# The low parts of streamed weights: a DMA that adds onto rounded weights, in place of a subtraction on VectorE

## The chip, the cores and the metric

One core of one Trainium2 chip runs the whole program in one launch. The metric is the device time in microseconds of that launch; lower is better. The core has TensorE (PE; its weight loads are listed as PEld), VectorE (DVE), ScalarE (ACT), GpSimd (POOL) and SyncE (SP). SP and POOL are the two engines from which this kernel issues nearly all of its DMAs.

## The reference, cut to what matters

Two transformer-like blocks over 512 tokens of width 1024, all in float32:

```python
# block 1: chunked attention + pooled branch, gated, then a conv-gated feed-forward
h = rms_norm(x, norm_mix_pre)
q, k, v, u, gates = split(h @ w_in)
y_a = chunk_band_attention(q, k, v, rel_bias) @ w_attn_out
y_b = multiscale_pool(u, w_pool_group, pool_scale) @ w_pool_out
g_a, g_b = split(sigmoid(gates + b_gate))
x = x + rms_norm((g_a * y_a + g_b * y_b) @ w_o, norm_mix_post)
f = conv_gated_ffn(rms_norm(x, norm_ffn_pre), w_up, conv_w, conv_b, w_down)
x = x + rms_norm(f, norm_ffn_post)
# block 2: gated delta rule + differential attention side by side
proj = rms_norm_2(x, w_norm) @ w_in_2
o_a = gated_delta_rule_chunked(...)      # needs the inverse of (I + L) of each chunk
o_b = diff_attention(...)
x = x + concat(o_a, o_b) @ w_out_2
```

Every large product is weights (about 20 million float32 numbers in all) against 512 tokens.

## The kernel before, in words

**Products in three parts.** A float32 operand is split in two numbers of the type that TensorE multiplies fast (fp32r): `hi`, the rounded value, and `lo`, the value minus `hi`. A product is then three matmuls on the same PSUM bank, in the order hi·ahi, hi·alo, lo·ahi (`mm3`). So of each 128 rows of a weight piece, the low part is wanted by the third matmul.

**The weight stream.** All weights come in 157 pieces in the order of use (`weight_order`), most of them 128 x 1024 (512 KB), those of the down-projection 128 x 1024 and 128 x 896. A piece goes through three steps:

- `fetch` loads it from HBM into a raw tile on SP's queue; there are two raw tiles, so a load waits until the piece two before it has been split.
- `split_next` makes `whi` from the raw tile with ACT (`split_hi`, a copy that rounds) and `wlo` with DVE (`split_lo`, raw minus `whi`), and then calls `fetch` for the next load. There are four `whi` and four `wlo` tiles.
- `take` hands the pair to the products. `weights` takes a piece and calls `advance`, which starts the split of the piece two further on. The split is thus begun about when the piece two before it starts on TensorE.

Six pieces that follow a seam (`early`) are split in halves into other tiles, and seven of the last product's pieces are split in two unequal parts. The first two pieces of the program are split half by half while they arrive, by code of their own.

**What sets the order.** Each engine works through its instructions in the order in which they were issued. `Issue` keeps estimated times and runs the background tasks (generators) when their operands should have come; a task pauses while ACT or DVE is more than `SLACK` us ahead. The estimates decide only that order. On the chip, each instruction waits for its operands, and what stands behind it on its engine waits too.

**The beginning.** The first two pieces (`w_qk`) are multiplied as they and `x` arrive. The next pieces, four of `w_v`, come through the stream; each product with them is token-major (`gemm_tok`): 256 columns at a time, with k = 0 to 3 from one piece and k = 4 to 7 from the next, so both are wanted at once. Beside it `first_norm` squares `x` on ACT and sums it on DVE and POOL (`acc`), and five loads of `rel` are issued on POOL's queue.

**The seams.** Between the two halves of a block, and between the blocks, the norm needs a whole product. There `Seam.chain` works through the tokens in two halves, and `seam_products` multiplies what is ready. The chain uses DVE (three steps for each of 8 k), ACT and, for the sum of squares, POOL. Two pieces are split under the second half.

**POOL in block 2.** Each of two `gdn_pair` tasks inverts 16 x 16 triangular blocks by substitution: 30 short POOL instructions (`cb`, `xt`) that depend on one another and are issued all together. A DMA (`dx`) then carries the result on, and TensorE needs it. Also on POOL's queue: the eight stores of `x` to DRAM after the second seam, their reload (`xr`) before the last product, and the stores of the output.

Of the kernel before, what the change touches and what calls it, by code (L numbers as in the profile page):

```python
# [13 lines left out]
ALU = mybir.AluOpType  # L14
# [15 lines left out]
# block 2's projections in order: a and z are feature-major tiles, the others two heads token-major  # L30
UNITS = ["a6", "a10", "a4", "a1", "a8", "a7", "a3", "a5", "a2", "a9", "q1", "v0", "a0", "q0",
         "k0", "z5", "a11", "k1", "z3", "z0", "z2", "z4", "z1", "z6", "z7", "v1"]
# heads in the order in which the last product takes them: the first of them in all tiles, then the others
# [7 lines left out]
# issue order: a task goes on when its last results are LEAD us away, unless an engine has SLACK us of work  # L41
# [23 lines left out]
def weight_order():  # L65
    """(array, piece, first column, end) in the order of use"""
    o = []

    def add(name, i=None, a=0, b=None):
        o.append((name, i, a, b))  # L70

    for hp in range(4):
        add("w_qk", 2 * hp)
        add("w_qk", 2 * hp + 1)
        if hp == 0:
            for i in range(4):
                add("w_v", i)
    add("w_pg")
    for i in range(4):
        add("w_u", i)  # L80
    for m in range(KD):
        add("w_g", 2 * m)
        add("w_g", 2 * m + 1)
        add("w_ap", m)
    for m in range(KD):
        add("w_o", m)
    for i in range(2 * MF):
        add("w_up", i)
    for m in range(KD):
        for a, b in ((0, 8), (8, 15), (15, 22)):  # L90
            add("w_dn", m, a * P, b * P)
    for u in UNITS:
        if u[0] in "az":
            add("w2_" + u[0], int(u[1:]))
        else:
            add("w2_" + u, 0)
            add("w2_" + u, 1)
    for m in range(KD):
        add("w_out", m)
    return o  # L100
# [5 lines left out]
class Issue:  # L106
    """Order of issue. Each engine works through its instructions in the order in which they are issued;
    the times that are kept here, in us, are estimates and decide that order alone."""
# [45 lines left out]
    def issue(self, e, op, outs, ins, func=None):  # L154
        self.count += 1
        lat = {"PE": 0.2, "V": 0.13, "A": 0.13, "G": 0.13}[e]
        start = max(self.free[e], self.ready(*ins) + lat)
        if e == "PE":
            start = max(start, self.now)
        # one engine at a time works on a PSUM bank  # L160
        held = [self.bank.setdefault(x.name, {}) for x in (*outs, *ins) if x.space == PSUM]
        for d in held:
            start = max([start] + [t + 0.05 for o, t in d.items() if o != e])
        if func in TABLES and TABLES[func] != self.table:
            self.table = TABLES[func]
            start += 1.28
        t = start + self.cost(e, op, outs, ins)
        for d in held:
            d[e] = t
        self.free[e] = t  # L170
        if e == "PE":
            self.now = t
        self.done(outs, t + (0.05 if e == "PE" else 0.0))
# [16 lines left out]
    def step(self):  # L190
        """tasks whose results have come go on; between two yields a task's work is issued together"""
        for task in list(self.tasks):
            if task[0] > self.now + LEAD:
                continue
            if not task[2] and max(self.free["V"], self.free["A"]) > self.now + SLACK:
                continue
            self.mark = task[3]
            r = next(task[1], "end")
            if r == "end":
                self.tasks.remove(task)  # L200
            else:
                task[0], task[3] = self.now if r == 0 else self.mark, self.mark
# [13 lines left out]
class Engine:  # L216
    """An engine whose instructions are counted by an Issue."""
# [18 lines left out]
def kernel(ctx, tc, aps, out, dbg=None):  # L236
# [13 lines left out]
    # PSUM banks: of each kind the time at which a bank's last readers are done  # L250
# [21 lines left out]
    # ---- background tasks: generators; "yield" waits for what was just issued, "yield 0" does not  # L272
# [3 lines left out]

    def move(dst, src):
        """a transfer within the chip's memories"""
# [3 lines left out]
    def grab_all(tag, n):  # L282
        """PSUM banks whose last readers are done"""
# [70 lines left out]
    # ---- weight stream: fetched three pieces ahead, split two ahead  # L354
# [16 lines left out]
    def split_next():  # L371
        while not raws:
            yield
        key, raw, n = raws.pop(0)
        yield from after(raw)
# [7 lines left out]
        elif key[0] == "w_out" and key[1] < NPART:  # L383
            # the first heads' weights pass through, the others' stay
# [8 lines left out]
        else:  # L393
            hi = wp.tile([P, n], F32R, tag="whi", name="whi", bufs=4)
            lo = wp.tile([P, n], F32R, tag="wlo", name="wlo", bufs=4)
            split_hi(raw, hi)
            yield
            split_lo(raw, hi, lo)
        done.append((key, hi, lo))
        fetch()  # L400

    def take(name, i=None, a=0, b=None):
# [3 lines left out]
        until(lambda: done)  # L406
# [4 lines left out]
    def weights(*key):  # L411
        """the next piece of the stream"""
# [9 lines left out]
    def wcol(w, k):  # L422
        """the weights of one k, of a piece that may wait in two halves"""
        return w[k // 4][:, k % 4 * P:(k % 4 + 1) * P] if isinstance(w, list) else w[:, k * P:(k + 1) * P]

    def mm(ps, w, x, start, stop):
        """a slice of a large product; while its operands are on their way other work goes on"""
# [34 lines left out]
    def copy(dst, src, scale=None):  # L462
        """on the engine that is free first"""
# [7 lines left out]
    def scale_rows(t, r):  # L471
        """t[p, c] *= r[p, c]"""
# [21 lines left out]
    def rstd(acc, col, tbs):  # L494
        """col[token] = 1 / rms and the same spread over the partitions"""
# [10 lines left out]
    class Seam:  # L506
        """x += rms_norm(f) and the next operand x * g split in two parts, one half of the tokens at a
        time: the norm of the first half runs under the products of the second."""
# [61 lines left out]
    def project_norm(wkeys, hi, lo, gname, seam, gnext):  # L570
        """f = W^T act in 8 output tiles; wkeys(m) lists each tile's pieces and their k ranges"""
# [27 lines left out]
    # ------------------------------------------------------------------ block 1: mixer  # L599
    # the first two products begin while their operands arrive  # L600
# [16 lines left out]
    # the tensor engine's clock rises while it works  # L617
# [60 lines left out]
    def attn_item(h, qb):  # L678
        """scores and softmax of (head, 128 queries)"""
# [40 lines left out]
    def attn_values():  # L720
        """transposed probabilities times values, (head pair, 128 keys) at a time"""
# [46 lines left out]
    def stack_q(src):  # L768
        """two heads of 64 features: for each its high part and, in the other half of the partitions, its low part"""
# [9 lines left out]
    def stack_k(src):  # L779
        """for each of two heads its high part in both halves, and their low parts"""  # L780
# [10 lines left out]
    def score(ps, q, k, j, qs, n):  # L791
        """(q_hi + q_lo) k_hi, then q_hi k_lo"""
# [59 lines left out]
    # pooling branch  # L852
# [44 lines left out]
    # gates, branch outputs, their mix  # L897
# [45 lines left out]
    # ------------------------------------------------------------------ block 1: feed-forward  # L943
# [37 lines left out]
    def seam_products(sn, keys, finish):  # L981
        """the first products after a seam, one half of the tokens at a time"""
# [72 lines left out]
    # inverses of the blocks of 16 x 16 go into zeros  # L1055
# [11 lines left out]
    # ------------------------------------------------------------------ block 2  # L1067
# [8 lines left out]
    def delta_gates():  # L1076
        """decays and write strengths, column c * 4 + h"""
# [74 lines left out]
    def gdn_pair(hs):  # L1152
        """two heads of the delta rule; chunks of 128 tokens. k, q and v carry a factor 2 from silu."""
# [12 lines left out]
        def decays():  # L1166
            """the chunks' running log decays on all partitions"""
# [41 lines left out]
        # the diagonal blocks of 64 x 64 of the chunks: [128, NT, 64], rows 0-63 one block, rows 64-127 the other  # L1209
        BLOCKS = ((LOW, LOW), (HIGH, HIGH))  # L1210
        halves = lambda t: t[:, :256].rearrange("p (c d) -> p c d", c=NT)
        # L passes through DRAM, where its diagonal blocks of 16, 32 and 64 lie at even distances
# [3 lines left out]
        def diag(t, n, row, w):  # L1216
            """of each of the diagonal blocks of n x n the rows from row on and w columns: [chunk, block, row, column]"""
# [38 lines left out]
        # off the inverse's path: values, keys and attention weights of the chunks  # L1256
# [46 lines left out]
        # inverse of I + L: 16 x 16 diagonal blocks by substitution, one block to a partition, then three merges  # L1303
# [31 lines left out]
        def inverse(i):  # L1335
            # T: transposed inverse of the blocks, D: the inverse, both compact
# [107 lines left out]
    def finish_head(o, ssq, idx, eps, nq=None):  # L1444
        """rms norm over the head, weight, silu(z), split: o is token-major [128, NT, 128]"""
# [29 lines left out]
    def tok_unit(nm, half_):  # L1475
        """token-major projection of two heads (256 columns): two [128, 2, 256] tiles of token blocks"""
# [26 lines left out]
    def v_unit():  # L1503
        """token-major values of the first two heads with the delta rule's b and a"""
# [21 lines left out]
    def rope_norm(nm, tok_):  # L1526
        """rms norm over 64 (its factor returned for q, applied for k) and rotation, in place"""
# [122 lines left out]
    # the residual waits in DRAM until the last product  # L1650
# [38 lines left out]
    def out_part(ps, w, a, b, cs=FULL, start=True, stop=True):  # L1689
        """the heads in places a to b"""  # L1690
# [20 lines left out]
    # the first heads in all tiles, then the last heads; three tiles wait in PSUM, the others' sums go to the residual  # L1711
# [29 lines left out]
def _pack(inputs):  # L1741
# [4 lines left out]
    def tiles(w):  # L1746
        """[K, N] -> [N/128, 128, K] pieces: one output tile's weights, k tiles side by side."""
# [3 lines left out]
    def tok_pieces(w, n):  # L1751
        """[1024, m*n] -> [m, 2, 128, 4*n]: token-major operands, half of k in each piece."""
# [94 lines left out]
```

## Time and profile before

| | |
|---|---|
| timed runs | 1040.13, 1041.13, 1042.51 us (median 1041.13) |
| profiled execution, from its first to its last instruction | 1042.7 us; the page gives no other time for it |
| TensorE busy, weight loads busy | 1024.7 us (98%), 849.2 us (81%) |
| VectorE, ScalarE, GpSimd busy | 684.9 us (66%), 499.5 us (48%), 74.5 us (7%) |
| DMA | 97.19 MB, mean 93 GB/s |

Busy times of the engines overlap and don't add up to the span. TensorE's matmuls are pipelined and their ends are modelled, so 98% says that TensorE is almost never without work and not how fast it goes. A wait is listed as the idle time of an engine, with what ended it. Issuing a DMA isn't counted as busy time.

### The profile page before, as it was taken

The numbers are of one execution on the slowest core, as the hardware profiler recorded it, in microseconds if no ns is written. First come the engines' busy times: TensorE is split into PE (matmuls) and PEld (weight loads), VectorE is DVE, ScalarE is ACT, GpSimd is POOL, SyncE is SP. The second block draws the span as 40 slices with busy tenths as digits, with TensorE's granted clock in tenths as the row PEclk, the third lists the DMA queues.
The fourth block names the chain that finished last, engine by engine and source line by source line (L and its number), as shares of the span: only waits on it lengthen the run. The fifth ranks groups of instructions, "written<-read, shape, count | busy, mean of one in ns | idle before, by whom it ended". The sixth has DMA issues, their size and how long they took to land. (4 is left out here: it accounts for less than half of the span.)

```text
span 1042.7 us, 15097 instructions
## 1 busy us (share of the span) xinstructions
PE 1024.7 (98%) x5718; PEld 849.2 (81%) x5718; DVE 684.9 (66%) x1409; ACT 499.5 (48%) x1039; POOL 74.5 (7%) x146
## 2 busy tenths in 40 slices
PE   8999999999999999999999999999999989999998
PEld 7966678888888888888888888898899978887876
DVE  6576774444447897766776522359885687997873
ACT  6566643333244554434434421334456674667670
POOL 3000000000002200000001000004100450001001
PEclk9999999999999999999999999999999998999999
DMA  7321122332332133233233323330533530023212
GB/s 261 133 71 49 63 70 92 102 96 88 100 110 73 61 102 101 82 100 101 90 94 116 102 85 112 91 122 8 177 102 107 143 92 22 21 62 122 70 53 81
DMA packets 40345, 97.19 MB, mean 93 GB/s; under 512 B 12160, under 2 KB 16528, under 8 KB 40272
## 3 DMA queue, kind: packets, MB, share of 16 engines
q1 hardware_dynamic: 37392, 87.53, 26.7%
q0 software_dynamic: 2736, 8.66, 2.4%
q8 instruction: 45, 0.74, 0.3%
q14 instruction: 28, 0.23, 0.1%
q10 hardware_dynamic: 144, 0.03, 0.0%
HBM read 90.29 MB, written 5.91 MB: 92 GB/s over the span
## 5 line engine op out<-in xcount | busy, mean ns | idle before, releaser
L230 DVE TENSOR_TENSOR wlo<-w,whi 128x1024 fp32r<-128x1024 f32 (+4 forms) x153 | 180.5, 1185 | 63.7 <-ACT whi L230 63.7
L230 PE MATMUL mm<-nh,whi 128*128 128x512 f32 x448 | 177.5, 396 | 0.0
L230 PE MATMUL mm<-nl,whi 128*128 128x512 f32 x448 | 177.4, 396 | 0.0
L230 PE MATMUL mm<-nh,wlo 128*128 128x512 f32 x448 | 177.2, 395 | 0.0
L230 ACT ACTIVATE whi<-w 128x1024 fp32r<-128x1024 f32 (+4 forms) x153 | 154.9, 1017 | 40.3 <-DMA w<-w_dn 22.0
L230 PEld LDWEIGHTS mm<-nh,whi 128*128 128x128 f32 x448 | 84.3, 188 | 18.5 <-issue 0.8
L230 PEld LDWEIGHTS mm<-nh,wlo 128*128 128x128 f32 x448 | 84.3, 188 | 18.3 <-issue 0.2
L230 PEld LDWEIGHTS mm<-nl,whi 128*128 128x128 f32 x448 | 84.3, 188 | 18.0 <-issue 0.2
L230 PE MATMUL mm<-h,whi 128*128 128x512 f32 x208 | 83.5, 402 | 0.0
L230 PE MATMUL mm<-h,wlo 128*128 128x512 f32 x208 | 83.3, 400 | 0.0
L230 PE MATMUL mm<-l,whi 128*128 128x512 f32 x208 | 83.2, 400 | 0.0
L230 PE MATMUL mm<-gh,whi 128*128 128x512 f32 (+1 forms) x198 | 73.0, 369 | 0.0
L230 PE MATMUL mm<-gh,wlo 128*128 128x512 f32 (+1 forms) x198 | 72.8, 368 | 0.0
L230 PE MATMUL mm<-gl,whi 128*128 128x512 f32 (+1 forms) x198 | 72.8, 368 | 0.0
L230 ACT ACTIVATE y<-hu,par 128x512 f32<-128x512 f32 x40 | 32.6, 814 | 65.6 <-DVE hu L230 65.6
L230 DVE SCALAR_TENSOR_TENSOR y<-hu,par,y 128x511 f32<-128x511 f32 x80 | 59.8, 748 | 1.4
L230 POOL TENSOR_TENSOR acc<-acc,sq 128x256 f32<-128x256 f32 (+1 forms) x31 | 26.2, 846 | 426.0 <-ACT sq L230 425.9
L230 DVE TENSOR_TENSOR hu<-mm,nb 128x512 f32<-128x512 f32 x40 | 27.6, 690 | 42.2 <-PE mm L230 42.2
L230 PE MATMUL mm<-wlo,nh 128*128 128x256 f32 (+1 forms) x192 | 55.3, 288 | 0.0
L230 PE MATMUL mm<-whi,nl 128*128 128x256 f32 (+1 forms) x192 | 55.0, 287 | 0.0
L230 PE MATMUL mm<-whi,nh 128*128 128x256 f32 (+1 forms) x192 | 55.0, 286 | 0.0
L230 DVE TENSOR_TENSOR acc<-acc,sq 128x512 f32<-128x512 f32 (+1 forms) x21 | 14.3, 682 | 49.9 <-ACT sq L230 49.8
(343 smaller groups left out, 2203.2 us busy)
## 6 DMA issues: line engine op xcount, KB each, us to landing
w<-w_up SPq DMA_DIRECT2D x44, 512.0 KB, 3.5
w<-w_g SPq DMA_DIRECT2D x16, 512.0 KB, 3.5
w<-w_dn SPq DMA_DIRECT2D x16, 448.0 KB, 3.4
w<-w_a SPq DMA_DIRECT2D x12, 512.0 KB, 3.5
w<-w_ap SPq DMA_DIRECT2D x8, 512.0 KB, 3.5
w<-w_o SPq DMA_DIRECT2D x8, 512.0 KB, 3.4
w<-w_dn SPq DMA_DIRECT2D x8, 512.0 KB, 3.6
w<-w_z SPq DMA_DIRECT2D x8, 512.0 KB, 3.8
```

The costliest lines, as they stand in the source:

```text
L230: return f(*args, **kw)
```

## The change

For the pieces that `split_next` handles whole, the low part is made in another way. ACT makes two passes over the raw tile: the first writes the rounded weights with their sign turned into `lo`, the second writes `hi` as before. Then a DMA on POOL's queue reads the same piece of the weights from HBM once more and adds it onto `lo`, so that `lo` becomes weights minus rounded weights. DVE's subtraction is gone for these pieces. The pieces of `early`, the seven divided pieces of the last product and the first two pieces of the program stay as they were.

Since the DMA is issued after a pause, a piece's place in the list `done` is now made when its split begins, and `take` waits until the place is filled. Comments and docstrings are also dropped, which changes no instruction.

```diff
+    def add(dst, src):
+        iss.load(dst, dst)
+        nc.gpsimd.dma_start(dst, src, accum_op=ALU.add)
+
...
         key, raw, n = raws.pop(0)
+        slot = []
+        done.append(slot)
         yield from after(raw)
...
             hi = wp.tile([P, n], F32R, tag="whi", name="whi", bufs=4)
             lo = wp.tile([P, n], F32R, tag="wlo", name="wlo", bufs=4)
+            split_hi(raw, lo, -1.0)
             split_hi(raw, hi)
             yield
-            split_lo(raw, hi, lo)
-        done.append((key, hi, lo))
+            name, i, a, b = key
+            src = aps[name] if i is None else aps[name][i]
+            add(lo, src[:, a:a + n])
+        slot += key, hi, lo
         fetch()
...
-        until(lambda: done)
+        until(lambda: done and done[0])
```

## Rows read from the trace of the kernel before

**Rows 1.** The page: busy us (share of the span) xinstructions of each engine.
```profile
PE 1024.7 (98%) x5718; PEld 849.2 (81%) x5718; DVE 684.9 (66%) x1409; ACT 499.5 (48%) x1039; POOL 74.5 (7%) x146
```
**Rows 2.** Groups of instructions by form: xcount | busy us, mean ns | idle before, its releaser.
```profile
L230 DVE TENSOR_TENSOR wlo<-w,whi 128x1024 fp32r<-128x1024 f32 x123 | 151.0, 1230 | 26.6 <-ACT whi L230 26.5
L230 ACT ACTIVATE whi<-w 128x1024 fp32r<-128x1024 f32 x123 | 129.1, 1051 | 14.7 <-DMA w<-w_a 6.0 <-DMA w<-w_up 4.8 <-PE mm L230 2.4
```
**Rows 3.** DMA queues (packets, MB, share of 16 engines), issues (KB, us to landing).
```profile
q1 hardware_dynamic: 37392, 87.53, 26.7%
...
w<-w_up SPq DMA_DIRECT2D x44, 512.0 KB, 3.5
...
rel<-rel POOLq DMA_DIRECT2D x8, 256.0 KB, 3.4
...
x<-x POOLq DMA_DIRECT2D x8, 256.0 KB, 6.1
```
**Rows 4.** Stretches: from:to us, length, busy (x) by engine, PEclk, DMA share, GB/s.
```profile
10.85:16.50 5.65, 5.65 (x26) 4.58 (x25) 4.08 (x6) 4.43 (x7) 0.00 (x0) 1.00 0.87 315
395.35:417.50 22.15, 22.15 (x98) 18.16 (x97) 15.53 (x20) 9.63 (x14) 0.00 (x0) 1.00 0.29 95
```
**Rows 5.** Time order, up-projection: start us, us, instruction [idle before <-releaser].
```profile
395.51 1.05 ACT L230 ACTIVATE whi<-w 128x1024 fp32r<-128x1024 f32 x1
...
406.56 0.69 DVE L230 TENSOR_TENSOR hu<-mm,nb 128x512 f32<-128x512 f32 x1 [0.86 <-PE mm L230]
```
**Rows 6.** Time order from 10 to 36 us, the second to fourth products.
```profile
10.85 0.93 SPq L275 DMA_DIRECT2D w<-w_v  x2
...
14.66 1.06 ACT L230 ACTIVATE whi<-w 128x1024 fp32r<-128x1024 f32 x1 [1.22 <-DMA w<-w_v]
...
15.75 1.23 DVE L230 TENSOR_TENSOR wlo<-w,whi 128x1024 fp32r<-128x1024 f32 x1 [1.49 <-ACT whi L230]
...
17.71 1.04 ACT L230 ACTIVATE whi<-w 128x1024 fp32r<-128x1024 f32 x1
...
17.89 1.30 POOL L230 TENSOR_TENSOR acc<-acc,sq 128x512 f32<-128x512 f32 x1 [16.61 <-ACT sq L230]
...
18.86 0.28 PE L230 MATMUL mm<-wlo,h 128*128 128x256 f32 x1
...
19.94 3.17 POOL L230 TENSOR_TENSOR acc<-acc,sq 128x512 f32<-128x512 f32 x2 [0.76 <-ACT sq L230]
...
20.32 0.39 PE L230 MATMUL mm<-wlo,h 128*128 128x256 f32 x1
...
23.06 2.81 POOL L275 DMA_DIRECT2D rel<-rel  x5
```
**Rows 7.** Waits of TensorE: who <- what ended it: us, times, longest.
```profile
PE s L230 <- DVE rsk L230: 3.5, 1, 3.5
```
**Rows 8.** Stretches around that wait (columns as in Rows 4).
```profile
858.00:860.00 2.00, 0.42 (x2) 0.28 (x2) 1.33 (x8) 1.20 (x4) 0.00 (x0) 0.78 0.55 124
...
864.00:866.00 2.00, 2.00 (x10) 1.83 (x9) 0.69 (x1) 0.00 (x0) 0.00 (x0) 0.51 0.00 0
866.00:868.00 2.00, 2.00 (x50) 1.74 (x49) 1.79 (x4) 0.86 (x3) 0.00 (x0) 1.00 0.02 4
```
**Rows 9.** Stretches of the two substitutions on POOL (columns as in Rows 4).
```profile
819.60:832.30 12.70, 12.70 (x80) 11.38 (x80) 9.96 (x28) 6.24 (x15) 10.40 (x30) 1.00 0.43 120
838.40:853.40 15.00, 14.72 (x185) 13.94 (x185) 12.88 (x21) 9.57 (x25) 12.70 (x30) 1.00 0.20 48
```
**Rows 10.** Time order: a split and the first use of its low part.
```profile
818.56 1.05 ACT L230 ACTIVATE whi<-w 128x1024 fp32r<-128x1024 f32 x1
...
831.22 0.39 PE L230 MATMUL mm<-nh,wlo 128*128 128x512 f32 x1
```
**Rows 11.** The second half of the first seam: the stretch.
```profile
342.60:356.20 13.60, 13.59 (x101) 12.52 (x102) 13.26 (x26) 7.22 (x16) 5.60 (x7) 1.00 0.06 11
```
**Rows 12.** DVE in time order, in that stretch.
```profile
352.47 2.89 DVE L230 TENSOR_TENSOR wlo<-w,whi 128x1024 fp32r<-128x1024 f32 x2
```

## The prediction

> **What bounds the kernel now.** I read the engines' shares first. TensorE is busy for 1024.7 of 1042.7 us, VectorE for 684.9, ScalarE for 499.5, GpSimd for 74.5 [rows 1]. So TensorE sets the time, and work that moves among the other three counts only where TensorE waits for it. Then the stretches: in the up-projection TensorE starts 98 matmuls in 22.15 us without a gap [rows 4]; at 24 matmuls a piece, a piece lasts 22.15 / 98 x 24 = 5.4 us, and the DMA engines are used at 0.29, that is 1.57 us a piece. Last I read, in time order, the places where TensorE uses a low part soon after it is made. The profiled execution's span is 1042.7 us, 1.6 us over the median of the timed runs (1041.13); the sum below is a difference, and I set it on the median.
>
> **The parts, one by one.**
>
> *VectorE.* Of 157 pieces, 142 change (157 less 2 at the start, 6 early, 7 divided). The 123 widest subtractions took 151.0 us [rows 2]; with 19 others at about 1.1 us each, VectorE loses 172 us and falls to 513 us (49%). In the up-projection that hides under TensorE and is worth nothing.
>
> *ScalarE.* One more pass of 1.05 us per piece [rows 2], 148 us in all: 648 us (62%). In the dense stretch it is busy 9.63 of 22.15 us [rows 4]; four more passes make it 13.9. That costs nothing there.
>
> *The DMA engines.* No row shows an adding DMA. It reads the weights and `lo` and writes `lo`: two reads where a load has one. Bounds in steady use are 1.57 us a piece (like a load) and 4.7 us (each access charged like a load). I take twice a load, 3.1 us, since the reads double and the write stays one. The share becomes 0.87 of a piece's 5.4 us: tight, but it fits.
>
> The Trainium skill, in "Collectives: The Full Stack", section "The bandwidth ceiling: the fold count and why AG ≠ RS ≠ AR", says that a reducing DMA puts two reads on the ring that a copy puts one on, and so runs at half the rate. By that rule the estimate is also 3.1 us a piece, and by the plain rate of the load rows 1.57; no run here shows it yet.
>
> *Latency of an add in steady use.* The split of a piece starts when the piece two ahead of it does: the pass at 395.51 belongs to a piece whose product begins about when the product before it is evacuated, at 406.56 [rows 5]. Of these 11 us one pass takes 1.05, so 9.9 remain. A load of 512 KB lands in 3.5 us; from POOL's queue 256 KB takes 3.4, and 6.1 in a burst of eight [rows 3]. I take 6 us for an add (3.5, plus 1.6 for the second read, plus about 1 for sharing the engines), between 3.5 and 9. It stays hidden. The next `fetch` waits for ScalarE's second pass and not for VectorE, which is no later.
>
> *The start: the firm loss.* Here the cover is missing. The first `w_v` piece lands just ahead of 14.66, ScalarE rounds it, VectorE subtracts by 16.98, and TensorE reads the low part at 18.86; of the second piece ScalarE starts at 17.71 and the low part is read at 20.32 [rows 6]. After the change the first add can be issued at 14.66 + 1.05 = 15.7. It costs POOL about 0.56 us to issue (five took 2.81 [rows 6]) and lands some 6 us after issue, because the DMA engines are at 0.87 in this stretch [rows 4]: at 21.7, so 2.8 us late. The second piece's pass starts one extra pass later, at 18.8, and ends at 19.8. Its add is issued between 19.8 and about 24, depending on whether it stands ahead of or behind the two `acc` sums on POOL that run from 19.94 for 3.17 us [rows 6] and wait themselves for squares on the delayed ScalarE. It lands between 25.8 and 30, against 20.32 + 2.8 = 23.1. The stall is 5.5 to 10 us in all, and I take 6.5, near the early end. Bounds: 3 us if both adds land like a plain load (23.3 against 20.32), 11 us if both stand behind sums and take 7 us. No other TensorE work is at hand.
>
> *The clock.* A wait of TensorE of 3.5 us [rows 7] was followed by a granted clock of 0.5 until 866, and 1.00 after it [rows 8]: the lower of the two levels, 1.2 GHz, for nearly 7 us, about 3.4 us of work lost. A stall of that length at the start would pay this as well; I put half of it, 1.5 us. Start: +8.
>
> *POOL's queue in block 2.* POOL runs its 30 substitution steps from 819.6 to 832.3 and again from 838.4 to 853.4 [rows 9]. An add that is issued behind the first row of steps is stuck for 12.7 us. One piece is split just then: its pass is at 818.56 and its low part is read at 831.22 [rows 10]. Issued ahead, its add lands near 826 and costs nothing; behind, it lands at 832.3 + 0.6 + 6 = 838.9, 7.7 us late. The pass ends at the moment when the steps begin, so I count half, +3.5 (0 to 11 with the clock). In the other direction, up to three adds ahead of the second row of steps cost it 0.56 us each, and TensorE's long wait [rows 7] follows from that row: up to +1.7, inside the range.
>
> *The seams: the gain.* In the second half of the first seam VectorE is busy 13.26 of 13.60 us, ScalarE 7.22 [rows 11], and two subtractions take 2.89 us of VectorE [rows 12]. Without them the chain for TensorE's operands is shorter, and ScalarE has room for two more passes. What is late next is the add of the first piece behind the seam, issued among POOL's sums (5.60 us busy [rows 11]). I take -1 us for each of two seams (0 to -2.9 each). The eight stores of `x` behind the second seam take 6.1 us to land [rows 3] and share a queue with the adds: 0 to +3, taken as 0.
>
> Sum: 8 + 3.5 - 2 = +9.5; 1041.13 + 9.5 = 1050.6 us. The likeliest case's own range is 1044 to 1060.
>
> **The rivals.**
>
> *VectorE was the hidden brake: faster.* For it: its 13.26 of 13.60 us in the seam. If both seams give all of 2.9 us, block 2 another 2, and the start costs its lower bound of 3, the time is 1041.1 - 5.8 - 2 + 3 = 1036.3. Against it: outside the start TensorE has little idle time to give back, as it is busy 98%. It decides from the point where the two adds at the start land within 5 us of the two passes.
>
> *All is hidden: no change.* Start at +3, POOL's queue at 0, seams at -3: 1041. Against it: the 2 us between the subtraction's end and the use at the start are less than any DMA's landing in the rows.
>
> *The DMA engines become the bound: much slower.* If an add takes more than 5.4 - 1.57 = 3.85 us of all engines, pieces come slower than TensorE uses them. At three times a load a piece takes 6.3 us, 0.86 more; over some 110 pieces of the dense stretches that is +95 us, 1145 with the start's loss. Against it: two reads are only twice. For it: no row shows the adder's own rate.
>
> **How the numbers follow.** Likeliest case (loss at the start and on POOL's queue) 0.58; DMA bound, in part or whole, 0.15; no change 0.13; faster 0.14. The range reaches to the fast case, 1036, and into the mild half of the DMA case, 1080. What a measurement of this kernel can tell from no change is about 0.2%, 2.1 us. Faster by more has 0.14, within it 0.13, slower by more 0.58 + 0.15 = 0.73.
>
> **What would show it.** Right: TensorE waits for the DMA onto `wlo` between 18 and 30 us, several us in all; issues on POOL's queue of 512 KB with a landing of 5 to 7 us; 142 more passes on ScalarE; a DMA share of 0.8 to 0.9 in the up-projection, where TensorE keeps 98 matmuls in about 22 us; a wait for an add near 831 us. Wrong: no wait at the start; adds that land in over 10 us, or TensorE's pace in the up-projection slower than 5.4 us a piece (the DMA case); seams shorter by more than the start is longer (the fast case).

## The result and the profile after

The changed kernel takes 1097.91 us (median of 4 runs, 1093.43 to 1101.09) against 1041.79 for the kernel before beside it: ratio 1.0522, 95% interval 1.0486 to 1.0558. It is 56 us slower. The prediction had the sign but said 1050.6, with a range that ends at 1080.

First the engines' shares of the changed kernel [rows 1]:

```profile
PE 1041.5 (95%) x5718; PEld 861.9 (79%) x5718; DVE 533.3 (49%) x1276; ACT 626.5 (57%) x1166; POOL 193.5 (18%) x288
```

TensorE runs the same 5718 matmuls. The span grew from 1042.7 to 1096.1, by 53.4 us, and that divides in two. (The times differ by 56.1: a time is some 1.8 us more than its span, 1097.86 against 1096.1, so the profiled execution of the kernel before was about 2.7 us longer than its median, and lateness read from the traces is against that execution.) TensorE is busy 16.8 us longer, though the work is the same: nearly all of that is matmuls at the lower clock (half of the busy time at a granted clock of 0.50 is 19.1 us, against 3.2 in the kernel before). And it stands 36.6 us longer (1096.1 - 1041.5 = 54.6 us idle, against 18.0 before). VectorE's busy time fell by 152 us and nothing came of it. (The subtractions' records add up to the predicted 172 us, but a busy time counts overlapping records once; copies of some 3 us also moved to it from ScalarE, as `copy` takes the engine that is free first. For the same reasons ScalarE's rose by 127 us and not by 148.)

The passes and the adds by form [rows 2]; the columns are as there:

```profile
L230 ACT ACTIVATE wlo<-w 128x1024 fp32r<-128x1024 f32 x123 | 129.2, 1050 | 10.7 <-DMA w<-w_a 2.5 <-PE mm L230 2.2 <-DMA w<-w_v 1.8
L230 ACT ACTIVATE whi<-w 128x1024 fp32r<-128x1024 f32 x123 | 128.7, 1046 | 0.0
...
L279 POOL DMA_DIRECT2D wlo<-w_up x41 | 35.4, 872 | 193.5 <-ACT wlo L230 185.7 <-ACT whi L230 7.8
```

ScalarE's extra pass costs the predicted 1.05 us. The record of an add on GpSimd is 0.87 us long, but the instruction behind it starts 0.54 to 0.61 us after the add's own start (at the start of the program, below, a sum at 22.47 behind the add at 21.86), so the 0.56 us taken for an issue holds. The page's queues and landings [rows 3]:

```profile
q0 software_dynamic: 23184, 81.84, 41.2%
q1 hardware_dynamic: 37392, 87.53, 24.1%
...
w<-w_up SPq DMA_DIRECT2D x44, 512.0 KB, 6.8
wlo<-w_up POOLq DMA_DIRECT2D x41, 512.0 KB, 7.7
```

The loads (q1) take 24.1% of 1096.1 us for 87.53 MB, 3.02 us a MB. The adds are what q0 gained, 41.2% less the 2.4% (25 us) of the kernel before's own 8.66 MB: 427 us for 73.2 MB, 5.83 us a MB. So 512 KB (0.524 MB) cost 1.58 us of all engines as a load and 3.06 as an add, 1.93 times; against a plain load on GpSimd's own queue (1.76 us in e5_copy, worked out alike) it is 1.74 times. The Trainium skill ("Collectives: The Full Stack", section "The bandwidth ceiling: the fold count and why AG ≠ RS ≠ AR") has a reducing DMA read twice and so run at half the rate of a copy; this case's traces agree in the main, with these factors of 1.93 and 1.74.

The dense stretch, TensorE's busy time and count in the third and fourth columns [rows 4]:

```profile
395.35:422.75 27.40, 27.40 (x121) 22.50 (x120) 15.55 (x23) 17.61 (x22) 4.55 (x6) 1.00 0.81 183
```

27.40 / 121 = 0.226 us a matmul, as before (22.15 / 98), without a gap at a DMA share of 0.81. Matmul by matmul (the n-th of the large products in one trace against the n-th in the other), the changed kernel is late by 22.8 us at the up-projection's start (389 us) and still by 22.8 at 610 us. The loss is made elsewhere, and TensorE's waits say where (who waits, for what: us in all, times, longest):

```profile
PE mm L230 <- DMA wlo<-w_k: 15.7, 2, 13.2
PE mm L230 <- DMA wlo<-w_v: 11.8, 5, 5.8
PE mm L230 <- DMA wlo<-w_a: 3.5, 2, 3.3
PE mm L230 <- DMA wlo<-w_up: 3.1, 1, 3.1
PE s L230 <- DMA T<-dx: 2.6, 2, 2.0
```

**The start** [rows 6], in time order:

```profile
14.58 1.06 ACT L230 ACTIVATE wlo<-w 128x1024 fp32r<-128x1024 f32 x1 [1.81 <-DMA w<-w_v]
...
15.97 1.05 POOL L279 DMA_DIRECT2D wlo<-w_v  x1 [14.69 <-ACT wlo L230]
...
21.86 0.88 POOL L279 DMA_DIRECT2D wlo<-w_v  x1
...
22.47 3.26 POOL L230 TENSOR_TENSOR acc<-acc,sq 128x512 f32<-128x512 f32 x2
...
23.70 0.58 PE L230 MATMUL mm<-wlo,h 128*128 128x256 f32 x1 [5.78 <-DMA wlo<-w_v]
...
37.07 0.60 ACT L230 ACTIVATE nb<-t 128x512 f32<-128x512 f32 x1 [14.43 <-PE t L230]
37.56 1.05 ACT L230 ACTIVATE wlo<-w 128x1024 fp32r<-128x1024 f32 x1
...
38.92 0.87 POOL L279 DMA_DIRECT2D wlo<-w_v  x1 [13.19 <-ACT wlo L230]
...
45.79 0.39 PE L230 MATMUL mm<-wlo,h 128*128 128x256 f32 x1 [2.32 <-DMA wlo<-w_v]
```

The first add is issued 0.3 us later than forecast and lands after 7.7 us, not 6. The third piece's passes stand on ScalarE behind `nb<-t` (the copy of the first norm's factors out of PSUM), which itself waits 14.4 us for the late TensorE, so its add is late too. Around the first wait the granted clock (the column after the five engines) is:

```profile
24.00:26.00 2.00, 2.00 (x10) 2.00 (x10) 0.83 (x2) 0.00 (x0) 1.65 (x2) 0.50 1.12 227
26.00:36.00 10.00, 9.06 (x42) 8.77 (x42) 2.34 (x13) 0.00 (x0) 0.00 (x0) 0.50 0.08 15
36.00:38.00 2.00, 2.00 (x19) 2.00 (x18) 0.30 (x1) 0.93 (x2) 0.00 (x0) 0.97 0.00 0
```

So 1.2 GHz for over 12 us after a wait of 5.8, and 42 matmuls in 10 us.

**Block 2** [rows 9, 10], the place of the longest wait:

```profile
860.38 1.05 ACT L230 ACTIVATE wlo<-w 128x1024 fp32r<-128x1024 f32 x1
...
862.80 1.05 ACT L230 ACTIVATE wlo<-w 128x1024 fp32r<-128x1024 f32 x1
...
877.12 1.79 POOL L279 DMA_DIRECT2D wlo<-w_k  x2 [0.29 <-issue]
...
884.12 0.58 PE L230 MATMUL mm<-wlo,nh 128*128 128x256 f32 x1 [13.22 <-DMA wlo<-w_k]
```

The passes of both `k1` pieces (weights for the keys of two heads) end at 861.43 and 863.85. Their adds stand in GpSimd's order behind the 30 substitution steps, which run from 863.04 to 876.8, and are issued at 877.12. The Trainium skill ("Perfetto Trace Analysis", section "Tensor Engine Instruction (MATMUL, LD_WEIGHTS)") calls GpSimd strictly first in, first out; the 16 and 13 us between the two ready passes and the issue agree with it.

**The first seam** [rows 11, 12]:

```profile
368.03 1.04 ACT L230 ACTIVATE wlo<-w 128x1024 fp32r<-128x1024 f32 x1
...
372.43 1.77 POOL L279 DMA_DIRECT2D wlo<-w_up  x2
...
377.98 0.80 PE L230 MATMUL mm<-nh,wlo 128*128 128x512 f32 x1 [3.07 <-DMA wlo<-w_up]
```

The pass ends at 369.07 and the add goes out at 372.43, behind GpSimd's last sums of the norm.

### The profile page after: what moved, and what is told of

Read it like the earlier page. It is cut to its first block, busy times and chain, and to the rows that moved or that the text cites. A ratio compares the mean times of both kernels' runs of the same rounds, so it can differ in the third digit from the quotient of the medians.

```text
span 1096.1 us, 15287 instructions
## 1 busy us (share of the span) xinstructions
PE 1041.5 (95%) x5718; PEld 861.9 (79%) x5718; DVE 533.3 (49%) x1276; ACT 626.5 (57%) x1166; POOL 193.5 (18%) x288
## 3 DMA queue, kind: packets, MB, share of 16 engines
q0 software_dynamic: 23184, 81.84, 41.2%
q1 hardware_dynamic: 37392, 87.53, 24.1%
## 4 chain that ended last, share of the span: by engine, by line
PE 71%; DMA 11%; issue 8%; DVE 4%; ACT 3%; POOL 2%; SPq 0%; POOLq 0%; ACTq 0%; DVEq 0%
PE mm L230 60%; PE t L230 5%; PE s L230 5%; DMA wlo<-w_v 2%; DMA wlo<-w_k 1%; DMA wlo<-w_dn 1%; DMA wlo<-w_a 1%; DMA wlo<-w_up 1%; DVE x L230 1%; POOL wlo L279 1%; DVE nl L230 1%; ACT wlo L230 1%; DMA wlo<-w_o 1%; DMA xt<-dl 1%; DVE f L230 1%
## 5 line engine op out<-in xcount | busy, mean ns | idle before, releaser
L230 PE MATMUL mm<-nh,wlo 128*128 128x512 f32 x448 | 179.8, 401 | 6.6 <-DMA wlo<-w_a 3.5
L230 ACT ACTIVATE wlo<-w 128x1024 fp32r<-128x1024 f32 (+1 forms) x142 | 147.2, 1037 | 37.6 <-DMA w<-w_dn 27.3
L230 PE MATMUL mm<-wlo,nh 128*128 128x256 f32 (+1 forms) x192 | 56.3, 293 | 18.6 <-DMA wlo<-w_k 15.7
L279 POOL DMA_DIRECT2D wlo<-w_up x41 | 35.4, 872 | 193.5 <-ACT wlo L230 185.7
L230 PEld LDWEIGHTS mm<-wlo,nh 128*128 128x128 f32 x192 | 37.3, 194 | 19.5 <-DMA wlo<-w_k 16.1
```

The source lines that it names most:

```text
L230: return f(*args, **kw)
L279: nc.gpsimd.dma_start(dst, src, accum_op=ALU.add)
```

## The experiments

The theory: an add costs nothing where its piece waits for TensorE, and costs much where TensorE waits for the piece (the start, behind the seams, block 2), and each such wait lets the clock fall. Rivals: ScalarE's passes; the adds' traffic; the planner's wrong idea of the landing; the adder's own slowness. Results as excess over the kernel before, run beside each; idle is the profiled span less TensorE's busy time (e13_fill's busy time holds its 5.6 us of idle work).

| kernel | excess, us | ratio (95%) | TensorE busy / idle, us |
|---|---|---|---|
| changed kernel | +56.1 | 1.0522 (1.0486-1.0558) | 1041.5 / 54.6 |
| e1_start | +36.8 | 1.0347 (1.0324-1.0369) | 1032.5 / 45.8 |
| e15_v01 | +43.3 | 1.0413 (1.0385-1.0441) | 1036.6 / 50.0 |
| e2_block2 | +23.8 | 1.0221 (1.0202-1.0240) | 1031.3 / 33.2 |
| e14_k1 | +39.8 | 1.0380 (1.0353-1.0408) | 1035.4 / 42.5 |
| e3_dense | +3.5 | 1.0031 (1.0018-1.0043) | 1024.6 / 19.4 |
| e16_dn | +2.1 | 1.0019 (1.0005-1.0032) | 1024.2 / 19.0 |
| e4_pass | +3.5 | 1.0027 (1.0013-1.0040) | 1027.0 / 17.6 |
| e5_copy | +26.5 | 1.0268 (1.0242-1.0294) | 1033.6 / 34.3 |
| e6_sub | +42.4 | 1.0428 (1.0390-1.0466) | 1037.4 / 42.4 |
| e7_sub_before | +8.9 | 1.0091 (1.0072-1.0109) | 1032.6 / 17.2 |
| e8_plan | +56.0 | 1.0532 (1.0507-1.0557) | 1041.6 / 56.2 |
| e9_lolast | +35.8 | 1.0351 (1.0326-1.0377) | 1032.2 / 44.7 |
| e10_lolast_before | +2.3 | 1.0023 (1.0008-1.0038) | 1027.0 / 17.6 |
| e11_lolast_dense | +3.6 | 1.0029 (1.0017-1.0042) | 1026.4 / 19.1 |
| e13_fill | +62.1 | 1.0588 (1.0557-1.0619) | 1044.1 / 57.6 |

### Undo the change by place

These six kernels differ from the changed one only in `keep` (cut; `...` stands for lines that only unpack `key` and set `keep` and `src`):

```diff
-            split_hi(raw, lo, -1.0)
...
+            if not keep:
+                split_hi(raw, lo, -1.0)
             split_hi(raw, hi)
             yield
...
-            add(lo, src[:, a:a + n])
+            if keep:
+                split_lo(raw, hi, lo)
+            else:
...
+                add(lo, src[:, a:a + n])
```

**e1_start**, `keep = name == "w_v"`. 

> The changed kernel with VectorE's subtraction kept for the first four streamed pieces (w_v), adds for the rest. Theory (the time goes where a low part is wanted sooner than an add can land, and in the half clock that follows such a wait): TensorE's waits for w_v up to 50 us and the 1.2 GHz stretches from 22 to 53 us go, 15 to 18 of the 56 us come back, so about 1081 us. Rival, the adds' traffic costs time everywhere: 4 of 142 adds gone, 2 us back, 1096. Rival, ScalarE's extra passes are the cost: the same 2 us.

19 us of the 56 came back, with 4 of 142 adds gone, a little more than the 15 to 18 expected. No wait for `w_v` is left before 50 us, nor a 1.2 GHz stretch before 333 us. Traffic and passes as causes would have given 2 us.

**e15_v01**, `keep = name == "w_v" and i < 2`. 

> The changed kernel with VectorE's subtraction kept for the first two w_v pieces, adds for the third and fourth and all others. Theory A (the first two pieces, next to the end of the cover of the first products, hold the loss, as the prediction had it): 11 to 14 us back, waits for w_v up to 50 us under 4 us, 1084 to 1087 us. Theory B (the third and fourth piece, which ScalarE splits late, hold what the first two give back, as with the idle matmuls): at most 7 us back, a wait of 4 to 6 us between 38 and 50 us, 1091 or more.

13 of the 19 us hang on the first two pieces (theory A). The third still makes TensorE wait (this row also holds a later `w_v`):

```profile
PE mm L230 <- DMA wlo<-w_v: 5.2, 2, 3.9
```

**e2_block2**, `keep = name.startswith("w2_") or name == "w_out"`. 

> The changed kernel with VectorE's subtraction kept for every piece of block 2 (all w2 pieces, and w_out), adds in block 1 alone. Theory (late low parts): TensorE's waits for w_a, w_v, w_q and w_k behind 720 us go, and the delay against the kernel before, 22 us at the second seam, stays 22 to 24 to the end: 1064 to 1067 us. Rival, the adds' traffic costs in proportion to their number: some 35 of 142 adds gone, 14 of 56 us back, 1084. Rival, the substitution steps on GpSimd are slowed by something else than the adds: the wait of 13 us stays and the time is over 1078.

32 us came back with 30 adds gone; the lateness against the kernel before stays at 21.7 us from the second seam to the end. The wait behind the substitution was the adds', not the steps' own.

**e14_k1**, `keep = name == "w2_k1"`. 

> The changed kernel with VectorE's subtraction kept for the two pieces of k1 alone, the ones whose adds stood behind the substitution steps on GpSimd. Theory A (that place alone holds most of block 2's loss): the 13.2 us wait and the half clock around it go, 14 to 18 us back, 1080 to 1084 us. Theory B (the wait only moves: the pieces next in line, a11 and z3, are then caught by the same steps): under 8 us back, 1090 or more.

Two adds of 142 hold 16 us. In place of the 13.2 us wait stands one of 3.1 for the substitution's result, nearly as long as the kernel before's own wait there [rows 7]:

```profile
PE s L230 <- DMA T<-dx: 3.3, 2, 3.1
```

**e3_dense**, `keep` for `w_v`, `w_up` 3 to 5, all `w2_` and `w_out`. 

> Adds only in the dense stretches: VectorE's subtraction kept for w_v, for the first three streamed pieces of the up-projection (3 to 5) and for all of block 2; some 95 pieces keep the add. Theory (late low parts at the start, behind the seams and in block 2 hold the whole loss): 1042 to 1046 us, no wait of TensorE over 1.5 us that the kernel before does not have. Rival, traffic or ScalarE's passes cost in proportion: two thirds of 56 us stay, about 1079.

Three quarters of the adds remain (105; the expectation's 95 was a miscount), and 3.5 of 56 us. That rules out traffic and passes as the main cost. What remains is met before 240 us (2.7 us late there), beside short waits for `w_qk` and `w_u` at 45 and 108 us.

**e16_dn**, `keep = name != "w_dn"`. 

> Adds for the pieces of w_dn alone (24 of 157), all else as in the kernel before. In e3_dense the delay against the kernel before fell from 3.5 to 2.1 us across the second seam, which those adds precede: this asks if that gain can be had without the losses. Theory: 1 to 2 us under the kernel before, 1041 to 1042.5. Rival (that drop is the order of issue and not VectorE's room): 1043 to 1045.

The theory's gain does not show: the rival's 1043 to 1045 holds (1045.1). In its trace it is 1.3 us ahead of the kernel before at 680 us and 0.6 us ahead at 720, past the second seam, so the adds of `w_dn` alone do not bring the drop that e3_dense has there. No kernel here beats the kernel before.

### One cost alone

**e4_pass**: the changed kernel with VectorE's subtraction in place of the add. It is the kernel before with the second pass, and with the early place in `done` that came with the change.

```diff
             split_hi(raw, hi)
             yield
-            name, i, a, b = key
-            src = aps[name] if i is None else aps[name][i]
-            add(lo, src[:, a:a + n])
+            split_lo(raw, hi, lo)
```

> The kernel before with ScalarE's second pass alone: the pass writes the weights of turned sign into the low part's tile, and VectorE's subtraction then overwrites it; no add. Theory (the adds' landing is the cost): the extra pass of 1.05 us delays each subtraction by as much, which shows at the start and behind the seams: 1043 to 1048 us. Rival, ScalarE's passes hold the loss: 1070 to 1098 us.

+3.5 us with 142 passes more: ScalarE's passes are not the loss, and neither is the early place in `done`, which this kernel and e16_dn (+2.1) have too.

**e5_copy**: `nc.gpsimd.dma_start(dst, src)` without `accum_op`. 

> The changed kernel with a plain load in place of each adding one (the low parts are then the weights themselves; this part of the computation is changed, all else is kept). Theory A (an add is dear because it reads twice): the transfers on GpSimd's queue take about half the engines' time, 1.6 us per 512 KB and not 3.05, land in 4 to 5 us and not 7 to 8, and the waits of TensorE shrink by some 2.5 us at each of about eight places: 1065 to 1080 us. Theory B (the place is the cost: two passes, an issue and any transfer behind one another, and GpSimd's order): the waits stay, 1088 to 1098. Under both the wait of 13 us behind the substitution steps stays at 10 or more.

Theory A, on size: 30 us less than with adds. On GpSimd's queue the page has:

```profile
q0 software_dynamic: 23184, 81.84, 25.3%
...
wlo<-w_up POOLq DMA_DIRECT2D x41, 512.0 KB, 4.0
```

Landing falls from 7.7 to 4.0 us, the record of an issue on GpSimd from 0.87 to 0.53, and the loads' landing from 6.8 to 4.6. The waits for `w_o`, `w_q` and the first `w_k` go. But 26.5 us of loss remain, with the longest waits at the same places:

```profile
PE mm L230 <- DMA wlo<-w_k: 7.9, 1, 7.9
PE mm L230 <- DMA wlo<-w_v: 6.7, 3, 3.3
```

So the adder's slowness holds about half of the loss, and even a low part that came by a plain load would be late at the start and behind the substitution. The expectation's 10 us or more behind the substitution was too high: 7.9.

**e6_sub** and **e7_sub_before**: `G.tensor_tensor` becomes `V.tensor_tensor` in the two lines of the substitution loop, in the changed kernel and in the kernel before.

> The changed kernel with the 2 x 30 substitution steps on VectorE, so that no add stands behind them on GpSimd. Theory: TensorE's wait of 13.2 us for w_k near 884 us falls to 1 to 3 us, and the 13.7 us at 1.2 GHz around it to 3.4 or none: 15 to 18 us back, about 1081 us. Rival (the wait is for the DMA engines, full of loads and adds there): it stays over 8 us, 1092 or more. Rival (the steps on VectorE hold up what VectorE does for TensorE): the time goes to the T<-dx and rsk waits, 1090 or more.

> The kernel before with the 2 x 30 substitution steps on VectorE, so that the run above can be read without the adds. Theory (the steps give the same there as here, their chain alone): between 4 us faster (the wait of 3.5 us and the half clock behind it go) and 2 us slower; 1038 to 1045 us. Rival (VectorE is the brake in that stretch): 1048 or more.

In e6 the wait behind the substitution falls from 13.2 to 0.2 us, further than the theory's 1 to 3; the other wait for `w_k` in this row, of 2.4 us, is that of an earlier piece, 2.5 us in the changed kernel:

```profile
PE mm L230 <- DMA wlo<-w_k: 2.6, 2, 2.4
```

13.7 us came back, a little less than the 15 to 18 expected. The move by itself cost the kernel before 8.9 us: the theory for e7 missed, and its rival's 1048 or more is what was measured. There the wait of rows 7 is gone, a row of 30 steps takes 7 us instead of 12.7, and the order of the work behind it changes. TensorE is idle no longer than before (17.2 us) but busy 7.9 us longer: it waits at another place, and 13.7 us at 1.2 GHz go with that wait. The lower clock explains 4.7 of the 7.9 us (half of the busy time at 0.50, less that of the kernel before):

```profile
975.69 0.87 PE L230 MATMUL t<-cst,e 128*128 128x128 f32 x3 [2.68 <-DVE e L230]
```

Whether the new order or VectorE's load put that wait there was not tested.

**e8_plan**: the planner is told of a later landing.

```diff
         iss.load(dst, dst)
+        iss.done([dst], iss.ready(dst) + 4.5)
```

> The changed kernel, with the planner told that an add lands 4.5 us later than it assumed (a plain load's time twice over). Nothing else is changed; the order of issue follows. Theory (there is no other TensorE work at hand at the late places): within 8 us of the changed kernel, 1088 to 1100. Rival (the planner's wrong landing time is the cause, and other work could fill the waits): under 1080.

No change in time, so a later landing in the planner's estimates gives nothing back. The waits change their places and names, as the planner orders other work ahead, which then waits too:

```profile
PE t L230 <- DVE acc L230: 15.3, 5, 7.9
PE mm L230 <- DMA wlo<-w_a: 10.1, 3, 5.9
PE mm L230 <- DMA wlo<-w_v: 6.4, 2, 3.9
```

### When the low part is wanted

**e9_lolast**, **e10_lolast_before**, **e11_lolast_dense**: in `gemm` (and alike in `gemm_tok`) the low parts come last.

```diff
...
-            mm3(ps, whi[:, sl], wlo[:, sl], ahi[k][:, cs], alo[k][:, cs], ...)
+            mm(ps, whi[:, sl(k)], ahi[k][:, cs], first and i == 0, False)
+            mm(ps, whi[:, sl(k)], alo[k][:, cs], False, False)
+        for i, k in enumerate(ks):
+            mm(ps, wlo[:, sl(k)], ahi[k][:, cs], False, last and i == len(ks) - 1)
```

> The changed kernel with each product's low-part matmuls behind its 16 others: a low part is wanted 16 x 0.226 = 3.6 us later in a product of 512 columns, 16 x 0.113 = 1.8 us later in a token-major one of 256. Theory (late low parts): the waits behind the seams, at w_o and at w_a go with the half clock behind them, those at w_v, w_q and w_k shrink by 1.8 us, the 13.2 us wait by 1.8: 12 to 20 us back, 1078 to 1086 us. Rival (traffic or ScalarE's passes): no more than 2 us back, 1096.

> The kernel before (VectorE's subtraction everywhere) with each product's low-part matmuls behind its 16 others. It tells how much of the 20 us that this order gave the changed kernel is the order itself. Theory (it only moves the moment when a low part is wanted, and no low part is late in the kernel before): 1038 to 1043 us. Rival (the order itself is better, as each weight tile's matmuls change less often or waits elsewhere shrink): under 1035.

> Adds only in the dense stretches (as in e3_dense) and the low-part matmuls behind the others. Theory: the small waits for w_o, w_qk and w_u (2.8 us in all) go, so 3 us under e3_dense's 1046.8: 1039 to 1044 us, within 0.3% of the kernel before. It is slower than 1046 only if the new order costs by itself (then e10_lolast_before shows the same).

The order alone is worth less than nothing (+2.3 us in the kernel before), and it gave the changed kernel 20 us: what helps is that the low part is wanted later, as the theory says. The waits did not shrink everywhere: those for `w_v` up to 50 us fell from 10.6 to 7.0 us, but those for `w_a` grew, from 4.5 to 8.3. In e9 GpSimd had the eight stores of `x` ahead of three `w_a` adds, the neighbour that the prediction took as 0:

```profile
PE mm L230 <- DMA wlo<-w_a: 5.1, 1, 5.1
```

e11 stayed at +3.6, so its expected 3 us did not come, though the waits for `w_qk` and `w_u` went and that for `w_o` fell to 0.2 us: the order costs about what they had cost, by e10. Adds in the dense stretches alone then cost 3.6 - 2.3 = 1.3 us, which is within the intervals.

### The clock

**e13_fill**: idle work in front of the first `w_v` low part.

```diff
+            if "fill" not in state:
+                state["fill"] = grab_now("t")
+                for _ in range(24):
+                    T.matmul(state["fill"], w0[0][0][:, :P], hhi[0], start=True, stop=True)
+                free(state["fill"])
```

> The changed kernel with 24 idle matmuls of 128x512 (24 x 0.23 = 5.5 us, into a PSUM bank that nobody reads) ahead of the first matmul that takes a w_v low part, so that TensorE works through its first wait of 5.8 us instead of standing. Theory (half of the loss at the start is the 13.7 us at 1.2 GHz behind that wait): no 1.2 GHz stretch from 22 to 36 us, the delay against the kernel before at 54 us falls from 17 to 10 to 12 us, the time by 4 to 7 us, to 1091 to 1094. Rival (the clock follows the wait's cause, or costs little, since TensorE waits for adds anyway): the same delay, 1096 to 1100.

The 1.2 GHz stretch behind the first wait is gone, as expected:

```profile
26.00:36.00 10.00, 9.27 (x77) 8.86 (x76) 4.28 (x17) 3.77 (x6) 0.87 (x1) 1.00 0.17 22
...
42.00:48.00 6.00, 0.76 (x7) 0.55 (x5) 0.00 (x0) 1.83 (x2) 0.85 (x1) 0.90 1.01 240
48.00:53.00 5.00, 5.00 (x24) 5.00 (x25) 0.00 (x0) 0.00 (x0) 0.00 (x0) 0.50 0.42 118
```

But the time did not fall. TensorE reached the fourth piece sooner, waited 5.2 us for its add (issued at 39.84) and met the low clock there; at 54 us it was 15.6 us late, not 10 to 12. So the fall of the clock follows from standing, and what it costs at the start is mostly time that would be waited for the next late add. That the whole kernel lost 6 us more than the changed one (62.1 against 56.1) is a miss. In its profiled execution matmuls follow each other more slowly even where nothing waits and the clock is at 1.00. In the up-projection, e13_fill and then the changed kernel:

```profile
500.00:560.00 60.00, 60.00 (x262) 48.82 (x261) 30.19 (x43) 35.79 (x44) 9.99 (x12) 1.00 0.80 186
...
500.00:560.00 60.00, 60.00 (x264) 49.16 (x263) 30.72 (x44) 34.47 (x42) 8.63 (x10) 1.00 0.83 197
```

From 395 to 620 us that is 981 matmuls against 988, or 0.7%, which over the whole kernel would be some 7 us. Why is open; so the lateness at 54 us is the part of this run that bears on the clock, and the total is not.

## Why the prediction was wrong

*Right.* TensorE bounds the kernel; what VectorE is spared hides (e3_dense: adds in the dense stretches give no gain). ScalarE's pass is 1.05 us and costs little (e4_pass). An add costs the DMA engines about twice a load, 3.06 us against 3.1 taken, and GpSimd the 0.56 us taken. The DMA engines fit at a share of 0.81 and the up-projection keeps its pace. The two places of loss that were named, the start and GpSimd's queue, hold some 36 of the 56 us (19 by e1_start, 16 by e14_k1).

*The failed step: the start, +8, measured 17 to 19.* "The stall is 5.5 to 10 us in all, and I take 6.5" was right for the two pieces it looked at: 5.78 + 0.94 = 6.7 us. It left out the third and fourth, which ScalarE splits only after `nb<-t`: 2.32 + 1.55 us more. They lie in the stretch that it read (10 to 36 us): in the kernel before the fourth's subtraction, at 32.35 for 1.22 us, ends only 0.9 us ahead of the use at 34.49. And "I put half of it, 1.5 us" for the clock was far too small: the matmuls from 23.7 to 36.1 us and from 46.4 to 53.2 ran at 1.2 GHz, some 16 us of busy time of which half, 8 us, is lost. 6.7 + 3.9 + 8 = 18.6, less the 1.1 us by which the first products began earlier: 17.5, and 16.9 is read at 54 us. These parts are not independent: in e13_fill, without the first stretch at 1.2 GHz, TensorE waits longer for the fourth piece and is only 1.3 us less late there.

*The failed step: GpSimd's queue in block 2, +3.5 (0 to 11), measured 16, and some 16 more in block 2 that the prediction had as hidden.* The mechanism was the right one and named, but "One piece is split just then" was a misreading. That piece's add went ahead of the steps, at 854.42, and cost nothing. The two `k1` pieces behind it are split inside the same row of steps, and that stands already in the trace of the kernel before, where the row runs from 819.6 to 832.3 [rows 9]. Their passes and the first use of their low part there:

```profile
825.73 1.06 ACT L230 ACTIVATE whi<-w 128x1024 fp32r<-128x1024 f32 x1
...
827.20 1.05 ACT L230 ACTIVATE whi<-w 128x1024 fp32r<-128x1024 f32 x1
...
837.00 0.28 PE L230 MATMUL mm<-wlo,nh 128*128 128x256 f32 x1
```

By the prediction's own landing of 838.9 they would have been 1.9 us late. They were 13.2 us late, since the row itself moved: it begins 7.9 us ahead of TensorE's need (863.04 against 870.90) and not 17.4 (819.6 against 837.0). Its input came later, as GpSimd waited for the DMA `xt<-dl` until then; what delayed that was not traced. With the clock this place holds 16 us (e14_k1). Of the 32 us that e2_block2 gave back, 16 are left. Most of them are what the part on steady use had as hidden: the pair of adds for a token-major product made TensorE wait 1.2 us for a `w_v`, 1.6 for a `w_q` and 2.5 for another `w_k` between 800 and 845 us, and 3.3 for a `w_a` behind the seam (next point); and the clock fell after the longer ones. This part is read from the waits; no run takes each of them away alone.

*The seams: -2, measured about +3.7 and +2.3.* The chain did get shorter, by little: across the first seam the lateness fell from 19.1 to 18.5 us, across the second from 24.0 to 22.2. Behind them it rose to 22.8 and 26.4. "What is late next" was named, the first piece's add behind GpSimd's sums, and then priced at nothing: it waited 3.4 us for its issue at either seam and gave 4.3 us behind the first (3.07 of waiting, the rest clock) and 4.2 behind the second (3.32 of waiting). 0 to -2.9 each had the wrong sign in its bounds.

*The clock* as a whole is some 16 of the 53.4 us of span (19.1 less 3.2). It was costed at one place; it fell at each of the longer waits.

*The rivals.* VectorE as the hidden brake gave 0.6 and 1.8 us at the seams, and the late adds behind them took more; the DMA engines as the bound are refuted by the up-projection. The range's upper end came from a share of that second rival, and the likeliest case's own range ended at 1060: neither had room for the first case's own terms at two to five times their size.

## What to carry to other kernels

Work that moves from a compute engine to a DMA turned 1.2 us into some 8 us of latency here, so cost it not where the weights stream but at each place where the stream starts anew: list every piece whose result is wanted sooner than the DMA lands, the third and fourth too, with what stands ahead of it on each engine in the new order, and for a queue behind a long row of steps, every piece that is split during the row. Price the lower clock behind every such wait. Where such waits stay, a later moment of need (low parts last) takes off some (20 of 56 us here); without them it is worth nothing.

## What the runs showed of the hardware

- An adding DMA of 512 KB from GpSimd took 3.06 us of all DMA engines (a load on SyncE's queue 1.58, a plain load from GpSimd in e5_copy 1.76) and 7.7 us in the median to land (a plain load 4.0, e5_copy); beside the adds the loads themselves landed in 6.8 us, against 3.5. Its record on GpSimd is 0.87 us long (a plain load 0.53), but the next instruction there starts 0.54 to 0.61 us after it.
- Two adds that were ready stood 16 and 13 us behind 30 short steps on GpSimd. The 30 steps took about 13 us there and 7.0 on VectorE (e7_sub_before).
- Around a wait of 5.8 us TensorE's granted clock was at 0.50 for 13.7 us; around waits of 2.7 to 3.6 us for 3.4 us in most cases, for 6.8 in some (the kernel before's 3.5, e2_block2's 3.2) and for 13.7 in two (3.3 us at the start of e5_copy, 2.7 us in e7_sub_before). With idle matmuls in place of the first wait it stayed at 1.00.
- At a DMA share of 0.81 and 183 GB/s, matmuls of 512 columns kept 0.226 us each.
